# Moving the gate biases into their column block and holding four weight sums behind the low part ahead of them

## The chip, the cores and the metric

The kernel runs on one NeuronCore of a Trainium2 chip. The metric is the device time of one execution in microseconds (us), taken as the median of the runs shown. A profile is one further execution with the hardware profiler on; it lists every instruction of the five engines: TensorE (PE in the rows, with its weight loads as PEld), VectorE (DVE), ScalarE (ACT), GpSimd (POOL) and SyncE (SP, which here only issues transfers).

## The reference, cut to what matters

The program is one layer of an encoder: a half-step feed-forward block, a gated mixer of attention and a Fourier branch, and a second half-step feed-forward block. The change lies in the gated mixer:

```python
u = _rms_norm(h, pre_g)
q, k, v, f, g = jnp.split(u @ w_in, SPLIT_POINTS, axis=-1)
...
y_attn = _blocked_gqa(q, k, v) @ w_attn_o
y_four = _fourier_mix(f) @ w_fourier
gates = jax.nn.sigmoid((g.reshape(b, s, N_BRANCHES, D_MODEL) + b_gate).astype(jnp.float32)).astype(h.dtype)
merged = gates[:, :, 0] * y_attn + gates[:, :, 1] * y_four
return h + _rms_norm(merged @ w_out, post_g)
```

There are 256 tokens, the width is 2048, and all is float32. The gates need `u @ w_in` for 4096 columns and the bias `b_gate`; the Fourier branch ends in a product with `w_fourier`.

## The kernel before, in words

**Products.** Every float32 weight is split into a high part (`whi`, a rounded copy made by ScalarE, line 105) and a low part (`wlo`, the weight minus the high part, made by VectorE, line 106). Each product is then three matmuls: high by high, low by high and high by low (lines 111 to 113). `split` keeps the last low-part instruction that was written down in `latest["V"]`. A weight piece is 128 by 1024 numbers: it is loaded into one of 5 buffers `raw`, and its parts go into rings of 6 buffers `hi` and `lo`.

**Column blocks.** `col_block` multiplies all tokens (two tiles of 128) by 512 columns: 16 steps `kk` of 6 matmuls, into two PSUM tiles `pc`. Other work is hung in between: a list `between`, spread evenly over the 16 steps, and a list `at` of pairs (step, work). `tc.issue_after(ins)` gives an order only: what is traced in the block on the engine of `ins` is queued behind `ins` on that engine, and nothing waits for `ins` to finish. Engines take their instructions strictly in the order in which the program holds them; that order is made beforehand by a scheduler that picks, engine by engine, what it thinks ready, the earlier written first.

**The mixer's middle.** There are eight gate blocks. Blocks 10 to 13 make the gate of the Fourier branch (`mB`), blocks 6 to 9 that of the attention (`zA`). `gate` runs a column block, loads 512 biases into `bg`, and then, for each of the two token tiles, VectorE computes `z` from `pc` and `bg` (line 1110) and ScalarE the sigmoid (line 1111).

A loop over `j` from 0 to 3 then does, in the order written: `gate(6 + j)` with other work hung in between (the Fourier transforms `fourier_parts` for j = 0, the query rotation for j = 1, and in all of them the transposes `turn_q`, whose results are split into `qTh` and `qTl`); `fourier_weights(j)`; `attn_scores` (products `sc`, then the row maximum `mx`, `nmx`, the exponentials `p` on ScalarE, `rinv`); `fourier_out(j)` (products `pf`); and the next query block, or a block of `w_ao` (products `pr`).

`fourier_weights(j)` prepares four weight pieces. For each, VectorE adds the two halves in place (line 1127), makes their difference from it (line 1128), and adds a multiple to `acc` (lines 1135 and 1137); the piece is split, and the ring keeps it until the `pf` matmuls have read it. `fourier_out(j)` needs all four pieces: 6 matmuls of each, then one with `wn` (line 1151) and two with the parts of `acc`.

For j = 0 the Fourier transforms inside the gate block need `zl`, the low part of `zs` (line 988 reads it).

Of the kernel before, what the change touches and what calls it, by code (L numbers as in the profile page):

```python
# [15 lines left out]
ALU = mybir.AluOpType  # L16
AX = mybir.AxisListType

P = 128
# [3 lines left out]
KD = D // P  # L23
F = 5632
NB = 512
# [34 lines left out]
def encoder_layer(  # L60
# [22 lines left out]
    V, A, T = nc.vector, nc.scalar, nc.tensor  # L83

    def load(dst, src):
        nc.sync.dma_start(dst, src)
# [4 lines left out]
    def work(name, shape=None):  # L91
        return wk.tile(shape or [P, NB], F32, tag="wk", name=name)

    def workr(name, shape=None):
        return wk.tile(shape or [P, NB], F32R, tag="wk", name=name)
# [6 lines left out]
    latest = {}  # L102

    def split(hi, lo, src):
        a = A.activation(hi, src, AF.Copy)  # L105
        v = V.tensor_tensor(out=lo, in0=src, in1=hi.bitcast(F32), op=ALU.subtract)  # L106
        latest["A"], latest["V"] = a.ins, v.ins

    def mm3(ps, lh, ll, rh, rl, first, last, onto=False):

        T.matmul(ps, lh, rh, start=first, stop=False, skip_group_check=onto)  # L111
        T.matmul(ps, lh, rl, start=False, stop=False, skip_group_check=onto)  # L112
        return T.matmul(ps, ll, rh, start=False, stop=last, skip_group_check=onto)  # L113
# [34 lines left out]
    def weights(src, spare=None):  # L148

        return [t for load_part in pieces(src, spare) for t in load_part()]  # L150
# [36 lines left out]
    def new_chunk(name):  # L187
        return (chunk.tile([P, 4, S], F32R, tag="ch_hi", name=name + "h"),
                chunk.tile([P, 4, S], F32R, tag="ch_lo", name=name + "l"))

    def new_u(t):
        return tuple(big(f"u{c}{t}", F32R, [P, KD, P]) for c in "hl")

    def col_block(u, w, nb, between=(), at=()):


        at = list(at)
        ps = [pmm.tile([P, NB], F32, tag="mm", name="pc") for _ in range(NT)]
        step = KD / (len(between) + 1)
        done = 0  # L200
        for kg in range(KD // CK):
            wt = weights(w[nb, kg])
            for k in range(CK):
                kk = kg * CK + k
                while at and kk >= at[0][0]:
                    with tc.issue_after(mm.ins):
                        at.pop(0)[1]()
                if done < len(between) and kk >= (done + 1) * step:
                    if between[done]:
                        with tc.issue_after(mm.ins):  # L210
                            between[done]()
                    done += 1
                for t in range(NT):
                    mm = mm3(ps[t][:], u[t][0][:, kk, :], u[t][1][:, kk, :], *wt[k], kk == 0, kk == KD - 1)
        return ps
# [146 lines left out]
    def cbs(a, cb):  # L362
        return a[:, cb * NB:(cb + 1) * NB]
# [413 lines left out]
    u = [new_u(t) for t in range(NT)]  # L777
# [89 lines left out]
    u, rs = nxt.u, nxt.rs  # L867
# [7 lines left out]
    def norm_rope(ps, nm, t):  # L875

        gc, gs = tabs[nm]
        q = work("q")
        ssq = small("ssq4", 4)
        heads = [slice(j * HD, (j + 1) * HD) for j in range(4)]  # L880
        for j, c in enumerate(heads):
            A.activation(q[:, c], ps[t][:, c], AF.Square, scale=rs[t][:, 0:1], accum_out=ssq[:, j:j + 1])
        r = rsqrt(ssq[:], 4, 1.0 / HD, "rh")
        V.tensor_scalar(out=r[:], in0=r[:], scalar1=rs[t][:, 0:1], scalar2=None, op0=ALU.mult)
        for j, c in enumerate(heads):
            A.activation(q[:, c], ps[t][:, c], AF.Copy, scale=r[:, j:j + 1])
        q3 = q[:].rearrange("p (j c) -> p j c", j=4)
        o = work("o")
        V.tensor_tensor(out=o[:].rearrange("p (j c) -> p j c", j=4), in0=q3,
                        in1=gc[:, t, :].unsqueeze(1).to_broadcast([P, 4, HD]), op=ALU.mult)  # L890
        tmp = work("tmp")
        for half in range(2):
            vo = tmp[:].rearrange("p (j a h c) -> p j a h c", j=4, a=2, h=2)[:, :, :, half, :]
            vi = q[:].rearrange("p (j a h c) -> p j a h c", j=4, a=2, h=2)[:, :, :, 1 - half, :]
            vg = gs[:, t, :].rearrange("p (a h c) -> p a h c", a=2, h=2)[:, :, half, :]
            V.tensor_tensor(out=vo, in0=vi, in1=vg.unsqueeze(1).to_broadcast([P, 4, 2, 32]), op=ALU.mult)
        V.tensor_tensor(out=o[:], in0=o[:], in1=tmp[:], op=ALU.add)
        return o
# [203 lines left out]

    def gate(nb, dst, cb, between=(), at=()):

        ps = col_block(u, w_in, nb, between=between, at=at)
        bg = work("bg")
        load(bg[:], b_gate[:, (nb - 6) * NB:(nb - 5) * NB].partition_broadcast(P))
        for t in range(NT):
            z = work("z")
            V.scalar_tensor_tensor(out=z[:], in0=ps[t][:], scalar=rs[t][:, 0:1], in1=bg[:], op0=ALU.mult, op1=ALU.add)  # L1110
            A.activation(cbs(dst[t], cb), z[:], AF.Sigmoid)
# [3 lines left out]
    def fourier_weights(cb):  # L1115


        acc = xpool.tile([P, NB], F32, tag="xt", name="acc")
        nraw, wn = xpool.tile([P, NB], F32, tag="xt", name="nraw"), workr("wn")
        load(nraw[0:NYR, :], w_fn[cb])  # L1120
        A.activation(wn[0:NYR, :], nraw[0:NYR, :], AF.Copy)
        V.tensor_tensor(out=wn[32:40, :], in0=nraw[32:40, :], in1=wn[32:40, :].bitcast(F32), op=ALU.subtract)
        forms = []
        for j in range(4):
            raw = wraw.tile([P, 2, NB], F32, tag="raw", name="raw")
            load(raw[:], w_fo[cb, j].rearrange("p (k c) -> p k c", k=2))
            V.tensor_tensor(out=raw[:, 0, :], in0=raw[:, 0, :], in1=raw[:, 1, :], op=ALU.add)
            V.scalar_tensor_tensor(out=raw[:, 1, :], in0=raw[:, 1, :], scalar=-2.0, in1=raw[:, 0, :],
                                   op0=ALU.mult, op1=ALU.add)
            hi = wring.tile([P, 2, NB], F32R, tag="hi", name="whi")  # L1130
            lo = wring.tile([P, 2, NB], F32R, tag="lo", name="wlo")
            split(hi[:], lo[:], raw[:])
            forms.append((hi, lo))
            if j == 0:
                V.tensor_scalar(out=acc[:], in0=raw[:, 0, :], scalar1=dcol[:, j:j + 1], scalar2=None, op0=ALU.mult)
            else:
                V.scalar_tensor_tensor(out=acc[:], in0=raw[:, 0, :], scalar=dcol[:, j:j + 1], in1=acc[:],
                                       op0=ALU.mult, op1=ALU.add)
        ready[cb] = acc, nraw, wn, forms
# [30 lines left out]
    for k in range(F_AHEAD):  # L1170
        load_f(k)
    kro = []
    gate(10, mB, 0, between=[lambda b=b: fold_tokens(b) for b in range(1, 4)]
         + [lambda t=t: kro.append(norm_rope(pk, "k", t)) for t in range(NT)])
    pq = col_block(u, w_in, 0, at=folds_at(4))
    qs = []
    gate(11, mB, 1, at=folds_at(4), between=[lambda t=t: qs.append(norm_rope(pq, "q", t)) for t in range(NT)])
    gate(12, mB, 2, at=folds_at(4), between=[lambda t=t: turn_k(t) for t in range(NT)])
    gate(13, mB, 3, at=folds_at(4))

# [14 lines left out]
    for j in range(4):  # L1195
        ps, qT = {}, new_chunk("qT")
        turns = [lambda t=t: turn_q(qT, qs, t) for t in range(NT)]
        if j == 0:
            ahead = fourier_parts() + turns
        elif j == 1:  # L1200
            qs = []
            ahead = [lambda t=t: qs.append(norm_rope(pq, "q", t)) for t in range(NT)] + [None] * 2 + turns
        else:
            ahead = turns
        gate(6 + j, zA, j, between=ahead)
        fourier_weights(j)
        for t in range(NT):
            attn_scores(j, qT, t, ps)
        fourier_out(j)
        oT[j] = new_chunk("oT")  # L1210
        parts = attn_parts(j, ps, oT[j])
        if j < 3:
            pq = col_block(u, w_in, j + 1, between=parts)
        if j in (1, 2):
            qs = []
            row_block(oT[j - 1], w_ao, j - 1, yA, j == 1,
                      between=[None] + [lambda t=t: qs.append(norm_rope(pq, "q", t)) for t in range(NT)])
# [175 lines left out]
```

## Time and profile before

| what | value |
|---|---|
| median of 3 runs | 1999.6 us (1998.6 to 2001.35) |
| profiled execution, its own time | 2000.01 us |
| its span in the trace | 1997.9 us |
| what lies around the span | 2.1 us |
| PE busy | 1983.4 us, 99% |
| DVE busy | 1776.0 us, 89% |
| ACT busy | 1301.3 us, 65% |

Busy times are sums over the instructions of an engine. The times at the left of timeline rows are microseconds from the start of the span. "Granted clock" is the TensorE clock as a share of full speed. In a wait row the arrow points from the waiter to what released it. In the loop over `j`, the four stretches in which PE goes from the gate block to the scores begin at about 923, 986, 1062 and 1143 us.

### The profile page before, as it was taken

To read this page: it belongs to the slowest core of one execution; us is meant where nothing else is said; L and a number is where in the kernel's file an instruction comes from. 1 tells how busy PE (TensorE), PEld (TensorE's weight loads), DVE (VectorE), ACT (ScalarE), POOL (GpSimd) and SP (SyncE) were. 2 spreads that over 40 slices of the span, in tenths; PEclk is the share of its full clock that TensorE was granted. 3 is DMA by queue.
4 is the path that set the end of the run, shared out by engine and by line. 5 is a ranking of instruction groups with operands and counts; after the bars stand their busy time and mean duration, and the time that the engine had idled before them with its cause. 6 is when DMAs were issued, how large, how long until landed. Compare 5 with 4: busy or idle time off the path is not lost.

```text
span 1997.9 us, 25756 instructions
## 1 busy us (share of the span) xinstructions
PE 1983.4 (99%) x9146; PEld 1644.7 (82%) x9146; DVE 1776.0 (89%) x2306; ACT 1301.3 (65%) x1860; POOL 84.8 (4%) x94
## 2 busy tenths in 40 slices
PE   9999999999999999999999999999999999999998
PEld 7888888888888888888888888888888888888886
DVE  6999999999999878886877885878999999999996
ACT  7566766767666756556666564656667766677666
POOL 0000000000000010100000000000000000000002
PEclk9999999999999999999999999999999999999999
DMA  9657766677668796854555557565577766677673
GB/s 328 222 177 237 227 221 204 207 242 224 227 203 277 241 302 202 252 181 142 192 193 186 193 166 276 195 216 194 177 230 232 232 209 208 216 232 232 215 259 127
DMA packets 117584, 434.19 MB, mean 217 GB/s; under 512 B 12840, under 2 KB 18992, under 8 KB 106064
## 3 DMA queue, kind: packets, MB, share of 16 engines
q1 hardware_dynamic: 103888, 411.65, 60.4%
q0 software_dynamic: 13568, 20.91, 6.0%
q8 instruction: 71, 1.16, 0.2%
q14 instruction: 57, 0.47, 0.1%
HBM read 409.44 MB, written 6.29 MB: 208 GB/s over the span
## 4 chain that ended last, share of the span: by engine, by line
PE 98%; DVE 1%; DMA 1%; ACT 0%; issue 0%; SPq 0%; DVEq 0%; ACTq 0%
PE pc L112 20%; PE pc L111 20%; PE pc L113 20%; PE pr L113 11%; PE pr L112 11%; PE pr L111 11%; PE pt L184 2%; PE pe L111 0%; PE pe L113 0%; PE pf L112 0%; PE pf L111 0%; PE pf L113 0%; DVE wlo L106 0%; PE pe L112 0%; PE pt L1081 0%; DMA raw<-in_f_gate 0%
## 5 line engine op out<-in xcount | busy, mean ns | idle before, releaser
L106 DVE TENSOR_TENSOR wlo<-raw,whi 128x1024 fp32r<-128x1024 f32 (+1 forms) x567 | 680.7, 1219 | 96.2 <-ACT whi L105 94.1
L105 ACT ACTIVATE whi<-raw 128x1024 fp32r<-128x1024 f32 (+1 forms) x567 | 586.5, 1053 | 252.3 <-PE pc L113 96.1
L112 PE MATMUL pc<-wlo,fh 128*128 128x512 f32 x738 | 287.6, 390 | 0.0
L113 PE MATMUL pc<-whi,fl 128*128 128x512 f32 x738 | 287.6, 390 | 0.0
L111 PE MATMUL pc<-whi,fh 128*128 128x512 f32 x738 | 287.4, 389 | 0.0
L111 PE MATMUL pc<-whi,uh 128*128 128x512 f32 x688 | 271.6, 396 | 1.2 <-ACT uh L838 1.2
L113 PE MATMUL pc<-whi,ul 128*128 128x512 f32 x688 | 269.7, 392 | 0.0
L112 PE MATMUL pc<-wlo,uh 128*128 128x512 f32 x688 | 269.3, 392 | 0.1
L105 ACT ACTIVATE whi<-t 128x1024 fp32r<-128x1024 f32 (+1 forms) x198 | 171.5, 866 | 138.6 <-DVE t L586 133.6
L586 DVE TENSOR_TENSOR t<-raw 128x512 f32<-128x512 f32 (+1 forms) x252 | 208.9, 841 | 14.2 <-DMA raw<-in_f_gu 10.5
L111 PE MATMUL pr<-whi,hTh 128*128 128x512 f32 x544 | 213.6, 393 | 0.0
L113 PE MATMUL pr<-whi,hTl 128*128 128x512 f32 x544 | 212.0, 390 | 0.0
L112 PE MATMUL pr<-wlo,hTh 128*128 128x512 f32 x544 | 211.9, 390 | 0.0
L106 DVE TENSOR_TENSOR wlo<-t,whi 128x1024 fp32r<-128x1024 f32 (+1 forms) x198 | 193.4, 977 | 13.6 <-ACT whi L105 13.3
L105 ACT ACTIVATE w<-raw 128x1024 fp32r<-128x1024 f32 x144 | 151.9, 1055 | 40.4 <-DVE raw L586 35.2
L106 DVE TENSOR_TENSOR w<-raw,w 128x1024 fp32r<-128x1024 f32 x144 | 175.5, 1219 | 0.0
L112 PEld LDWEIGHTS pc<-wlo,fh 128*128 128x128 f32 x738 | 138.6, 188 | 29.1
L111 PEld LDWEIGHTS pc<-whi,fh 128*128 128x128 f32 x738 | 138.6, 188 | 29.0
L113 PEld LDWEIGHTS pc<-whi,fl 128*128 128x128 f32 x738 | 138.6, 188 | 28.8
L111 PEld LDWEIGHTS pc<-whi,uh 128*128 128x128 f32 x688 | 129.7, 188 | 27.9 <-ACT uh L838 2.7
L112 PEld LDWEIGHTS pc<-wlo,uh 128*128 128x128 f32 x688 | 129.6, 189 | 26.8 <-DVE wlo L106 1.7
L113 PEld LDWEIGHTS pc<-whi,ul 128*128 128x128 f32 x688 | 129.4, 188 | 27.0
(350 smaller groups left out, 3183.4 us busy)
## 6 DMA issues: line engine op xcount, KB each, us to landing
raw<-in_f_down SPq DMA_DIRECT2D x176, 512.0 KB, 5.2
raw<-in_f_gu SPq DMA_DIRECT2D x144, 512.0 KB, 4.5
raw<-in_f_gu SPq DMA_DIRECT2D x72, 1024.0 KB, 7.4
raw<-in_w_in SPq DMA_DIRECT2D x112, 512.0 KB, 4.4
raw<-in_f_up SPq DMA_DIRECT2D x32, 512.0 KB, 5.0
raw<-in_w_ao SPq DMA_DIRECT2D x32, 512.0 KB, 3.8
raw<-in_w_out SPq DMA_DIRECT2D x32, 512.0 KB, 4.9
raw<-in_f_gate SPq DMA_DIRECT2D x31, 512.0 KB, 5.8
```

What stands on the lines that cost most here:

```text
L105: a = A.activation(hi, src, AF.Copy)
L106: v = V.tensor_tensor(out=lo, in0=src, in1=hi.bitcast(F32), op=ALU.subtract)
L111: T.matmul(ps, lh, rh, start=first, stop=False, skip_group_check=onto)
L112: T.matmul(ps, lh, rl, start=False, stop=False, skip_group_check=onto)
L113: return T.matmul(ps, ll, rh, start=False, stop=last, skip_group_check=onto)
L184: T.transpose(pt[:, j, :], src[:, j * P:(j + 1) * P], ident[:])
L586: V.tensor_tensor(out=out, in0=a, in1=b, op=ALU.subtract)
```

## The change

Two edits. In `gate`, the load of the biases and the allocation of its buffer are written down inside the column block, at step 8 of 16, and no longer behind it. In `fourier_weights`, the sum of the two halves of each piece is queued on VectorE behind the low-part instruction that was written down last before it (`latest["V"]`). For the first piece of a block that is the last split that was traced inside the gate block; for the other three it is the low part of the piece before. The lines from 1127 on are one line further down in the changed kernel: 1127 becomes 1128, 1128 becomes 1129, 1135 becomes 1136, 1137 becomes 1138, 1150 becomes 1151.

```diff
     def gate(nb, dst, cb, between=(), at=()):
 
-        ps = col_block(u, w_in, nb, between=between, at=at)
         bg = work("bg")
-        load(bg[:], b_gate[:, (nb - 6) * NB:(nb - 5) * NB].partition_broadcast(P))
+        bias = (KD // 2, lambda: load(bg[:], b_gate[:, (nb - 6) * NB:(nb - 5) * NB].partition_broadcast(P)))
+        ps = col_block(u, w_in, nb, between=between, at=sorted([*at, bias], key=lambda a: a[0]))
...
             load(raw[:], w_fo[cb, j].rearrange("p (k c) -> p k c", k=2))
-            V.tensor_tensor(out=raw[:, 0, :], in0=raw[:, 0, :], in1=raw[:, 1, :], op=ALU.add)
+            with tc.issue_after(latest["V"]):
+                V.tensor_tensor(out=raw[:, 0, :], in0=raw[:, 0, :], in1=raw[:, 1, :], op=ALU.add)
             V.scalar_tensor_tensor(out=raw[:, 1, :], in0=raw[:, 1, :], scalar=-2.0, in1=raw[:, 0, :],
                                    op0=ALU.mult, op1=ALU.add)
```

**Place 1: VectorE in the first steps of gate block 6 (j = 0).** The rows run from the two `z` of the block before it to the first low parts of the Fourier transform. Before:

```order
L1110 SCALAR_TENSOR_TENSOR z<-pc,r1r,bg 128x512
L106 TENSOR_TENSOR wlo<-raw,whi 128x1024
L1127 TENSOR_TENSOR raw<-raw 128x512
L106 TENSOR_TENSOR zl<-zs,zh 128x260
L1128 SCALAR_TENSOR_TENSOR raw<-raw 128x512
L106 TENSOR_TENSOR wlo<-raw,whi 128x1024
```

Now:

```order
L1110 SCALAR_TENSOR_TENSOR z<-pc,r1r,bg 128x512
L106 TENSOR_TENSOR wlo<-raw,whi 128x1024
L106 TENSOR_TENSOR zl<-zs,zh 128x260
L106 TENSOR_TENSOR wlo<-raw,whi 128x1024
L106 TENSOR_TENSOR al<-pa,ah 126x260
```

The first sum (line 1127) stood between a low part and `zl`; it and all that follows from it have left this place.

**Place 2: VectorE at the end of gate block 6, from the two `z` on.** Before, the four pieces are done by then, and the rows are scores work and the low parts of the next block's weights:

```order
L106 TENSOR_TENSOR qTl<-pt,qTh 128x4x128
L1110 SCALAR_TENSOR_TENSOR z<-pc,r0r,bg 128x512
L1110 SCALAR_TENSOR_TENSOR z<-pc,r1r,bg 128x512
L1060 TENSOR_REDUCE mx<-sc 128x2
L106 TENSOR_TENSOR wlo<-raw,whi 128x1024
L1122 TENSOR_TENSOR wn<-nraw,wn 8x512
L1061 TENSOR_SCALAR nmx<-mx 128x2
```

Now:

```order
L1110 SCALAR_TENSOR_TENSOR z<-pc,r1r,bg 128x512
L1122 TENSOR_TENSOR wn<-nraw,wn 8x512
L1128 TENSOR_TENSOR raw<-raw 128x512
L1060 TENSOR_REDUCE mx<-sc 128x2
L1129 SCALAR_TENSOR_TENSOR raw<-raw 128x512
L1136 TENSOR_SCALAR acc<-raw,dcol 128x512
L1061 TENSOR_SCALAR nmx<-mx 128x2
L106 TENSOR_TENSOR wlo<-raw,whi 128x1024
L1128 TENSOR_TENSOR raw<-raw 128x512
L1129 SCALAR_TENSOR_TENSOR raw<-raw 128x512
L1138 SCALAR_TENSOR_TENSOR acc<-raw,dcol,acc 128x512
L1068 RECIPROCAL rinv<-rsum 128x2
```

All four pieces, with their sums, differences, `acc` and low parts, now stand behind the two `z`, one piece after the other. For j = 1 it is the same, but that the first sum and difference stand just ahead of the two `z`. On PE the `pf` matmuls keep their place behind three of the four scores products.

**Place 3: VectorE at the end of gate block 9 (j = 3; block 8 is alike).** Before:

```order
L1137 SCALAR_TENSOR_TENSOR acc<-raw,dcol,acc 128x512
L106 TENSOR_TENSOR wlo<-raw,whi 128x1024
L106 TENSOR_TENSOR qTl<-pt,qTh 128x4x128
L1150 SCALAR_TENSOR_TENSOR acc<-nraw,dcol,acc 8x512
L106 TENSOR_TENSOR wlo<-raw,whi 128x1024 x2
L1110 SCALAR_TENSOR_TENSOR z<-pc,r0r,bg 128x512
```

Now:

```order
L1128 TENSOR_TENSOR raw<-raw 128x512
L1129 SCALAR_TENSOR_TENSOR raw<-raw 128x512
L1138 SCALAR_TENSOR_TENSOR acc<-raw,dcol,acc 128x512
L1151 SCALAR_TENSOR_TENSOR acc<-nraw,dcol,acc 8x512
L106 TENSOR_TENSOR wlo<-raw,whi 128x1024
L1110 SCALAR_TENSOR_TENSOR z<-pc,r0r,bg 128x512
```

The four pieces still stand ahead of the two `z`, but now behind the last low part of the gate's own weights; the whole fourth piece, with its sum, now stands between the second `qTl` and the first `z`.

## The prediction

> **What bounds the kernel now.** I read the page first: busy times, then the chain that ended last.
>
> ```profile
> span 1997.9 us, 25756 instructions
> PE 1983.4 (99%) x9146; PEld 1644.7 (82%) x9146; DVE 1776.0 (89%) x2306; ACT 1301.3 (65%) x1860; POOL 84.8 (4%) x94
> PE 98%; DVE 1%; DMA 1%; ACT 0%; issue 0%; SPq 0%; DVEq 0%; ACTq 0%
> ```
>
> TensorE sets the end: 98% of the chain is its own work. Only 1997.9 − 1983.4 = 14.5 us of the span are left to win on it, and every wait given to it lengthens the program one for one. VectorE at 89% has little slack as a mean, so the stretch decides. The table by stages gives, for each window, its length, the busy time of PE, PEld, DVE, ACT and POOL, the granted clock, the DMA share and GB/s; the first row holds gate block 6, the second the scores and `pf` behind it, the third the query block, gate block 7 with its `pf`, and what follows:
>
> ```profile
> 882.00:925.00 43.00, 41.21 (x223) 34.53 (x223) 30.43 (x45) 19.71 (x36) 0.00 (x0) 0.96 0.43 139
> 925.00:960.00 35.00, 35.00 (x179) 29.20 (x178) 26.14 (x38) 26.00 (x56) 0.00 (x0) 1.00 0.55 184
> 960.00:1050.00 90.00, 90.00 (x433) 74.78 (x432) 74.12 (x135) 62.27 (x121) 0.00 (x0) 1.00 0.57 189
> ```
>
> PE loses 1.8 us in the first window and nothing in the others. VectorE has 12.6 us free of 43 inside gate block 6 and 8.9 of 35 behind it. What the waits of PE and of `z` name there (number, us in all, longest):
>
> ```profile
> PE pa L988 <- DVE zl L106: 1.8, 1, 1.8
> DVE z L1110 <- DMA bg<-in_b_gate: 1.4, 2, 1.0
> ```
>
> **Part 1, the biases: 0.** The same number of loads is issued on SP's queue, earlier. It removes at most the 1.4 us that `z` waited for them in all. During both waits PE had other work: its second window shows it full at 35.00 of 35.00 just behind such a `z`. So I take 0; the bounds are −1.4 and +1.0, the latter if a transfer put ahead makes a weight late by one such wait.
>
> **Part 2, place 1: −3.5 us.** VectorE there, then the PE row that waited, then the two windows before and behind it:
>
> ```profile
> 887.23 1.23 DVE L106 TENSOR_TENSOR wlo<-raw,whi 128x1024 fp32r<-128x1024 f32 x1
> 889.94 0.69 DVE L1127 TENSOR_TENSOR raw<-raw 128x512 f32<-128x512 f32 x1 [1.49 <-DMA raw<-in_w_fo]
> 890.55 0.42 DVE L106 TENSOR_TENSOR zl<-zs,zh 128x260 fp32r<-128x260 f32 x1
> 891.49 1.22 DVE L106 TENSOR_TENSOR wlo<-raw,whi 128x1024 fp32r<-128x1024 f32 x1
> 892.62 0.68 DVE L1127 TENSOR_TENSOR raw<-raw 128x512 f32<-128x512 f32 x1
> 893.34 0.69 DVE L1128 SCALAR_TENSOR_TENSOR raw<-raw 128x512 f32<-128x512 f32 x1
> 893.95 0.68 DVE L1127 TENSOR_TENSOR raw<-raw 128x512 f32<-128x512 f32 x1
> 891.02 0.33 PE L988 MATMUL pa<-odd,zl 128*126 128x130 f32 x1 [1.77 <-DVE zl L106]
> 888.38:891.79 3.41, 1.64 (x13) 1.29 (x13) 1.92 (x5) 1.22 (x2) 0.00 (x0) 1.00 0.77 257
> 891.79:895.21 3.42, 3.42 (x16) 3.12 (x16) 3.35 (x5) 1.08 (x3) 0.00 (x0) 0.50 0.41 155
> ```
>
> The first sum waited for its transfer, and `zl` stood behind it. In the changed order `zl` follows the low part of 887.23 at once and is done by about 888.9, ahead of 891.02 − 1.77 = 889.25, where PE began to wait. So 1.77 us go. The window behind the wait ran at half the clock, 3.42 × 0.5 = 1.7 us of work lost; that goes with it. Together −3.5; bounds 0 (something else becomes late there) and −3.5.
>
> **Part 2, place 2, j = 0: +11.1 us.** Before, this preparation lay inside the gate block, under PE's 16 steps. Now all of it is behind the two `z`, and `pf` needs it. Rows of VectorE, of PE and of ScalarE:
>
> ```profile
> 916.45 2.33 DVE L1137 SCALAR_TENSOR_TENSOR acc<-raw,dcol,acc 128x512 f32<-128x512 f32 x3
> 920.56 0.73 DVE L1150 SCALAR_TENSOR_TENSOR acc<-nraw,dcol,acc 8x512 f32<-8x512 f32 x1
> 922.68 0.69 DVE L106 TENSOR_TENSOR qTl<-pt,qTh 128x512 fp32r<-128x512 f32 x1
> 923.29 0.74 DVE L1110 SCALAR_TENSOR_TENSOR z<-pc,r0r,bg 128x512 f32<-128x512 f32 x1
> 923.95 0.74 DVE L1110 SCALAR_TENSOR_TENSOR z<-pc,r1r,bg 128x512 f32<-128x512 f32 x1
> 924.61 0.68 DVE L1060 TENSOR_REDUCE mx<-sc 128x2 f32<-128x512 f32 x1
> 925.21 1.21 DVE L106 TENSOR_TENSOR wlo<-raw,whi 128x1024 fp32r<-128x1024 f32 x1
> 923.24 0.28 PE L111 MATMUL sc<-kT,qTh 128*128 128x256 f32 x1
> 925.39 0.40 PE L111 MATMUL pf<-whi,foTh 128*128 128x512 f32 x1
> 925.62 0.40 PE L112 MATMUL pf<-wlo,foTh 128*128 128x512 f32 x1
> 931.71 0.39 PE L1151 MATMUL pf<-wn,mids 72*128 72x512 f32 x1
> 931.95 0.39 PE L111 MATMUL pc<-whi,uh 128*128 128x512 f32 x1
> 926.98 1.06 ACT L105 ACTIVATE whi<-raw 128x1024 fp32r<-128x1024 f32 x1 [0.87 <-PE pf L113]
> ```
>
> Count from the first `z` (0 = 923.29), with distances from one row to the next where two follow each other: `z` 0.66 each, `mx` 0.6, sum 0.72 to its own difference and difference 0.61 to the next (the three rows around 893), `acc` 2.33 / 3 = 0.78, a low part 1.13 (891.49 to 892.62), a high part 1.06. Two `z` and `wn` (like `mx`) end at 1.9, the first sum at 2.5; `mx` stands next, so the difference ends at 3.9, the high part at 5.0, the first low part at 6.2. From then a piece costs 0.72 + 0.61 + 0.78 + `rinv` or `nmx` 0.1 + `mx` 0.6 + low part 1.14 = 4.0; the high part (1.06) lies under `acc` and `mx` (1.38), so it costs nothing, but if ScalarE is late with it (a table load stands in its queue) each piece grows by up to 1.3. The fourth has `acc` of line 1150 too, 0.73. The fourth low part ends at 6.2 + 4.0 + 4.0 + 4.7 = 18.9, and behind it PE has still some four matmuls of `pf` (0.23 apart) and the one of `wn`: the query block starts at 20.05. Before, PE went from the first score to that block in 931.95 − 923.24 = 8.7 us, 8.9 with one matmul that the changed order pulls ahead. The difference is **11.1**. Below: all of `mx` and `rinv` fall between pieces without delay, −2. Above: 4 × 1.3 = +5.
>
> Queued behind it on VectorE are the low parts of the query block. They need PE's 20.05 at the earliest and are 1.13 each against 2.7 us of PE (12 matmuls) for a weight piece: no term. The four buffers `raw` come free at 6 to 19, so the weights after next land late by as much, but the nearest that depends on the last is wanted some ten microseconds behind the start of the query block: no term either; what a late transfer would cost goes into the upper end.
>
> **Part 2, place 2, j = 1: +8.9 us.** The same, with the first sum and difference ahead of `z`: first low part at 2.5, second 7.9 (its high part waits for the difference, ending at 5.6, and VectorE for both), third 11.9, fourth 16.6, query block 17.8; less 8.9. Bounds −2 and +4 around it.
>
> **Part 2, place 3, j = 2 and j = 3: +2.0 and +2.8.** Here the pieces stay ahead of `z`, but begin behind the last low part of the gate's weights. Rows of VectorE, of PE (the fourth scores product) and of ScalarE:
>
> ```profile
> 1048.11 1.22 DVE L106 TENSOR_TENSOR wlo<-raw,whi 128x1024 fp32r<-128x1024 f32 x1
> 1062.02 0.74 DVE L1110 SCALAR_TENSOR_TENSOR z<-pc,r0r,bg 128x512 f32<-128x512 f32 x1
> 1129.84 1.21 DVE L106 TENSOR_TENSOR wlo<-raw,whi 128x1024 fp32r<-128x1024 f32 x1
> 1142.49 0.74 DVE L1110 SCALAR_TENSOR_TENSOR z<-pc,r0r,bg 128x512 f32<-128x512 f32 x1
> 1068.94 0.39 PE L111 MATMUL sc<-kT,qTh 128*128 128x256 f32 x1
> 1149.40 0.39 PE L111 MATMUL sc<-kT,qTh 128*128 128x256 f32 x1
> 1063.59 1.28 ACT L1111 ACT_TABLE_LOAD   x1
> 1064.88 1.15 ACT L1111 ACTIVATE zA<-z 128x512 f32<-128x512 f32 x2
> 1065.94 0.62 ACT L1121 ACTIVATE wn<-nraw 72x512 fp32r<-72x512 f32 x1
> ```
>
> A piece is sum 0.72, difference 0.69, high part 1.06, low part 1.14, about 3.7 with the gaps; from the end of the gate's last low part, 1049.25, four of them, with `qTl` (0.7) under the last, put the first `z` at 1064.85, against 1062.02. ScalarE has the fourth high part, two of the next block (to 65.6), a table load, the sigmoids 1.15, `wn` 0.6, a second table load 1.3 and the two exponentials (0.9): done at 1070.9. The fourth scores product needs the buffer that they free and stood at 1068.94: **+2.0**. The same for j = 3 from 1131.0: `z` at 1146.1, against 1142.49, exponentials done at 1152.2 against 1149.40: **+2.8**. Bounds 0 (`acc` and the high parts overlap wholly) and 3 or 4.
>
> **The clock: +3.4.** One wait of 1.77 us was followed by one window of 3.42 us at 0.50. The waits at j = 0 and 1 are longer, so at least one such window each: 2 × 1.7. Bounds 0 and +8 (windows within the waits, and behind the 2-us waits at j = 2, 3: five in all).
>
> **Sum.** 11.1 + 8.9 + 2.0 + 2.8 + 3.4 − 3.5 + 0 = +24.7. The profiled execution took 2000.0 us (1997.9 of span and 2.1 around it), 0.4 over the median of the runs; so 1999.6 + 24.7 = 2024.
>
> **Rivals.**
> 1. *The clock stays at half while the waits recur.* Each piece's six matmuls (0.23 apart) are a burst of 1.4 us between waits of 2 to 3 us; if the gate counts the share of busy time, as the window with 1.64 of 3.41 us suggests, it stays at 0.50 from the first wait until a full window: the 8.7 us of PE work at each of j = 0, 1 then take up to twice as long, 17.4 us more, of which I leave a third to two thirds under the next wait: +7 to +12, 2031 to 2036. Against: the burst hides in the wait that follows it.
> 2. *The clock never falls.* Place 2 is no single wait of 11 us but four or five, cut by the bursts of a piece's matmuls; the longest by the steps above is 4.0 − 1.2 = 2.8 us. If such waits are too short for the gate, the clock term goes: −3.4, 2020.6. Against it stands the window at 0.50 behind a wait of 1.77 us. The Trainium skill, "TensorE: Matmul & The Clock Gate", section "Why this matters for your kernels", gives this rule: gaps of an idle PE above some 3 us are to be avoided, since one idle window takes the clock back to half. By it the clock stays full here; the trace disagrees, with 1.77 us before its slow window.
> 3. *Half of it.* VectorE takes ready work between the waits better than I chain it, or one of the two blocks is prepared in time because the engine reaches the held sum before `z` is ready: 2 × 10 goes to 10, 2011 to 2013. For j = 1 the sum's place ahead of `z` speaks for it; against it, that the second `qTl` at 922.7 leaves 0.6 us only.
> 4. *The other side: faster.* If the first sum runs at least 11 us before the first `z` in all four blocks (VectorE's 12.6 us free in the block would then take the four pieces), no `pf` waits and only place 1 counts: 1999.6 − 3.5 = 1996. It decides by where the second `qTl` stands; in the order it is directly ahead of the `z`.
> 5. *No change*: the waits at j = 2, 3 and the gain at place 1 cancel (2.0 + 2.8 − 3.5 = +1.3), with place 2 hidden as in 4.
>
> **How the numbers follow.** Forecast 0.57, rivals 0.15, 0.12, 0.08, 0.05, 0.03. A measurement tells from no change about 0.2%, 4 us: faster 0.05 (rival 4), same 0.03, slower 0.92. The summed bounds of the large terms are −4 and +9, with which the forecast itself reaches from 2016 to 2032; taking in rivals 1 and 2 and cutting rival 3, 2014 to 2034.
>
> **What would show it.** Right: PE's waits list `pf` (lines 111 and 112) behind `whi` and `wlo`, about 10 us at 921 to 942 and as much near 1000; the one of line 988 is gone; the windows behind 925 and near 1000 show PE some 10 us short of full, with a clock under 1.00 in the table of windows there; scores products of blocks 8 and 9 wait 2 to 3 us for `p`. Wrong: first sums that start long before the first `z`, or waits of `pf` under 5 us in a block. The bias rows should no longer release `z`, with no time coming of it.

## The result and the profile after

The changed kernel takes 2020.9 us in the median (2019.8 to 2022.4), against 1999.7 us before; the ratio is 1.0106 (95% interval 1.0091 to 1.0121), so 21.2 us slower, with 18 to 24 us in the interval. The prediction was 2024.

The page of the profiled execution of the changed kernel, in the same rows as before:

```profile
span 2019.8 us, 25750 instructions
PE 1992.9 (99%) x9146; PEld 1647.5 (82%) x9146; DVE 1777.3 (88%) x2306; ACT 1300.4 (64%) x1860; POOL 84.8 (4%) x94
PE 93%; DVE 4%; ACT 1%; DMA 1%; issue 0%; SPq 0%; DVEq 0%; ACTq 0%
```

The instructions that count as busy are the same in number on each engine (the six fewer in the span row are not among them) and VectorE's busy time is nearly the same; the chain that ended last now runs through VectorE for 4% of the span. PE's busy time has grown by 9.5 us though its matmuls are the same: that is mostly the lower clock. The rest of the 21.9 us of span is idle time. The waits of PE (what waited, for what: us in all, times, longest) say where:

```profile
PE pf L111 <- ACT whi L105: 10.3, 5, 3.0
PE pc L111 <- ACT whi L105: 2.0, 2, 1.0
PE pf L112 <- DVE wlo L106: 1.5, 3, 0.5
```

None of these was there before, and the wait of line 988 for `zl` is gone. The list names ScalarE's high parts first, but ScalarE is only the last link; for the first high part of j = 0 it waited itself, for VectorE's difference:

```profile
924.03 1.06 ACT L105 ACTIVATE whi<-raw 128x1024 fp32r<-128x1024 f32 x1 [2.00 <-DVE raw L1129]
```

In the timeline of VectorE behind the two `z` of gate block 6 one piece follows the other almost without a gap (lines as in the changed kernel, one more than before; only the second `qTl`, the first `z`, the four sums and the fourth low part are shown, the rows between them are left out):

```profile
919.35 0.69 DVE L106 TENSOR_TENSOR qTl<-pt,qTh 128x512 fp32r<-128x512 f32 x1 [2.52 <-ACT qTh L105]
919.96 0.74 DVE L1110 SCALAR_TENSOR_TENSOR z<-pc,r0r,bg 128x512 f32<-128x512 f32 x1
922.10 0.69 DVE L1128 TENSOR_TENSOR raw<-raw 128x512 f32<-128x512 f32 x1
926.26 0.69 DVE L1128 TENSOR_TENSOR raw<-raw 128x512 f32<-128x512 f32 x1
930.05 0.69 DVE L1128 TENSOR_TENSOR raw<-raw 128x512 f32<-128x512 f32 x1
934.05 0.68 DVE L1128 TENSOR_TENSOR raw<-raw 128x512 f32<-128x512 f32 x1
937.36 1.21 DVE L106 TENSOR_TENSOR wlo<-raw,whi 128x1024 fp32r<-128x1024 f32 x1
```

The first sum stands 2.1 us behind the first `z`, the sums are 4.2, 3.8 and 4.0 us apart, and the fourth low part ends at about 938.5, 18.5 us behind the first `z`. Ahead of the second `qTl` VectorE stood idle for 2.5 us: it waited for the `qTh` that this `qTl` reads, and the sums stand behind it in its order. PE, meanwhile (the longer waits):

```profile
925.14 1.22 PE L111 MATMUL pf<-whi,foTh 128*128 128x512 f32 x2 [2.92 <-ACT whi L105]
932.93 0.73 PE L111 MATMUL pf<-whi,foTh 128*128 128x512 f32 x2 [1.55 <-ACT whi L105]
936.92 0.73 PE L111 MATMUL pf<-whi,foTh 128*128 128x512 f32 x2 [1.54 <-ACT whi L105]
938.67 0.79 PE L111 MATMUL pc<-whi,uh 128*128 128x512 f32 x1 [1.01 <-ACT whi L105]
```

To see what each block cost, I compare one and the same matmul in both timelines of PE. Before (the first scores product of j = 0; a matmul of the query block behind j = 0; one of the column block behind j = 1; the fourth scores products of j = 2 and 3 stand in the prediction):

```profile
956.53 0.40 PE L112 MATMUL pc<-wlo,uh 128*128 128x512 f32 x1
1039.76 0.39 PE L112 MATMUL pc<-wlo,uh 128*128 128x512 f32 x1
```

and in the changed kernel, with the fourth scores products of j = 2 and 3 too:

```profile
919.91 0.28 PE L111 MATMUL sc<-kT,qTh 128*128 128x256 f32 x1
966.07 0.40 PE L112 MATMUL pc<-wlo,uh 128*128 128x512 f32 x1
1060.81 0.39 PE L112 MATMUL pc<-wlo,uh 128*128 128x512 f32 x1
1090.02 0.39 PE L111 MATMUL sc<-kT,qTh 128*128 128x256 f32 x1
1170.48 0.39 PE L111 MATMUL sc<-kT,qTh 128*128 128x256 f32 x1
```

The shifts are −3.3 at the first scores product (923.24 before), +9.5 behind j = 0, +21.1 behind j = 1, and +21.1 still at j = 2 (1068.94) and j = 3 (1149.40). Ahead of place 1 the changed kernel was already 0.3 us late (the first `z` of the block before gate block 6: 886.13 against 885.87). So place 1 gave 3.6 us, j = 0 took 12.9, j = 1 took 11.5, j = 2 and 3 took nothing. The last 0.8 us of the span's 21.9 came behind the loop over `j`, all of it near 1895 us in the second feed-forward block; single runs of one kernel lie 2 to 3 us apart, and I give it no cause.

The clock, in the table by windows of the changed kernel (length, busy time of PE, PEld, DVE, ACT and POOL, granted clock, DMA share, GB/s):

```profile
919.16:938.71 19.55, 11.48 (x49) 7.66 (x48) 18.49 (x33) 13.72 (x29) 0.00 (x0) 0.91 0.25 80
938.71:942.62 3.91, 3.91 (x10) 3.17 (x11) 3.66 (x5) 3.91 (x9) 0.00 (x0) 0.56 0.71 235
1006.99:1013.82 6.83, 6.22 (x15) 4.86 (x16) 6.40 (x11) 6.83 (x16) 0.00 (x0) 0.50 0.63 208
```

The first row holds all waits of j = 0; VectorE is busy for 18.5 of its 19.6 us. The second and third are the windows behind the last low part of j = 0 and j = 1: full or nearly full of matmuls, at about half the clock. By PE's busy time in them they lose 3.91 × 0.44 = 1.7 and 6.22 × 0.5 = 3.1 us, 4.8 together.

### The profile page after: what moved, and what is told of

Read it like the earlier page. It is cut to its first block, busy times and chain, and to the rows that moved or that the text cites. A ratio compares the mean times of both kernels' runs of the same rounds, so it can differ in the third digit from the quotient of the medians.

```text
span 2019.8 us, 25750 instructions
## 1 busy us (share of the span) xinstructions
PE 1992.9 (99%) x9146; PEld 1647.5 (82%) x9146; DVE 1777.3 (88%) x2306; ACT 1300.4 (64%) x1860; POOL 84.8 (4%) x94
## 4 chain that ended last, share of the span: by engine, by line
PE 93%; DVE 4%; ACT 1%; DMA 1%; issue 0%; SPq 0%; DVEq 0%; ACTq 0%
PE pc L112 19%; PE pc L111 19%; PE pc L113 19%; PE pr L113 10%; PE pr L112 10%; PE pr L111 10%; PE pt L184 2%; DVE wlo L106 1%; ACT whi L105 1%; PE pe L111 0%; PE pe L113 0%; DMA raw<-in_f_gu 0%; PE pe L112 0%; PE pt L1081 0%; DMA raw<-in_w_in 0%
## 5 line engine op out<-in xcount | busy, mean ns | idle before, releaser
L586 DVE TENSOR_TENSOR t<-raw 128x512 f32<-128x512 f32 (+1 forms) x252 | 208.9, 841 | 15.0 <-DMA raw<-in_f_gu 11.2
```

The source lines that it names most:

```text
L586: V.tensor_tensor(out=out, in0=a, in1=b, op=ALU.subtract)
```

## The experiments

**The two edits apart.** First the biases alone: the new `gate`, and `fourier_weights` as before.

```diff
-            with tc.issue_after(latest["V"]):
-                V.tensor_tensor(out=raw[:, 0, :], ...
+            V.tensor_tensor(out=raw[:, 0, :], ...
```

> Only the biases are moved; the first sums are not held. Theory: the biases price nothing, so 1999.7 us, within 2 us of before (the interval holds 1.000); the wait of PE for zl (1.8 us) and its window at half the clock stay, and no z waits for its biases. Rival: the earlier loads shift the weights behind them and carry a part of the loss, then over 2 us slower; or the 1.4 us of waits of z were paid by PE, then 1998.3 us.

Measured: 2000.4 us, ratio 0.9999 (0.9991 to 1.0008). The earlier load costs and brings nothing within 2 us. The wait for `zl` is there (1.4 us). Two details came out otherwise than expected: no window at half the clock follows that wait (the last section returns to this), and one `z` still waited 1.4 us for its biases.

Then the hold alone, with `gate` as before the change.

```diff
-        bg = work("bg")
-        bias = (KD // 2, lambda: load(bg[:], ...))
-        ps = col_block(u, w_in, nb, between=between, at=sorted([*at, bias], key=lambda a: a[0]))
+        ps = col_block(u, w_in, nb, between=between, at=at)
+        bg = work("bg")
+        load(bg[:], ...)
```

> Only the hold; the biases are loaded where they were before. Theory: all of the change's effect is here, 2020 to 2022 us, with the same waits of pf (about 12 us) as in the changed kernel. Rival: the two edits act together (the biases landing while VectorE is on the pieces), then under 2015 us.

Measured: 2020.6 us, ratio 1.0100 (1.0086 to 1.0113), with 9.4 us of waits of `pf` for high parts and 1.7 for low parts (10.3 and 1.5 in the changed kernel). The hold carries the whole effect.

**Block by block.** The sums are held in some blocks only; the biases stay moved. In the code of `fourier_weights`, `cb` is what the text calls j, the gate block from 0 to 3, and `j` is the piece.

```diff
-            with tc.issue_after(latest["V"]):
+            with tc.issue_after(latest["V"]) if cb >= 2 else contextlib.nullcontext():
```

> Biases moved, and the sums held in the last two gate blocks only (j = 2, 3). Theory after the trace of the changed kernel: the hold costs nothing there, 1999.7 us within 2 us, with the zl wait still there. Rival, the prediction's own terms: +2.0 and +2.8, 2004.5 us, with waits of the fourth scores product for the exponentials.

Measured: 2000.4 us, ratio 0.9999 (0.9990 to 1.0008), with no wait of the scores products. The prediction's terms for j = 2 and 3, 4.8 us together, lie outside this interval.

With `cb == 0` in place of `cb >= 2`:

> Biases moved, sums held in the first gate block alone (j = 0). Theory: that block's share as the trace of the changed kernel gives it, 12.9 us lost at the scores and pf less 3.6 us gained at zl, +9.3: 2009.7 us, with about 8 us of waits of pf. Rival: the waits of the second block are partly a consequence of the first (weights that land late), then this kernel carries more than 13 us; or the gain at zl is not real, then +12.9, 2013 us.

Measured: 2011.0 us, ratio 1.0051 (1.0038 to 1.0065), +10.3 us. The waits of `pf` are those of the first block alone:

```profile
PE pf L111 <- ACT whi L105: 6.0, 3, 2.9
PE pf L112 <- DVE wlo L106: 1.1, 2, 0.5
```

With `cb == 1`:

> Biases moved, sums held in the second gate block alone (j = 1). Theory: the two blocks add up, so this is the change (+21.2) less the run held at j = 0 alone (+11.6 by medians, +10.3 by the ratio): +9.6 to +11.5, 2009 to 2011 us, with about 6 us of waits of pf, and the zl wait there. Rival (the second block is worse because the first ran late): under 2007 us.

Measured: 2009.9 us, ratio 1.0044 (1.0030 to 1.0059), +8.8 us, a little under what was expected but with an interval (+6.0 to +11.8) that holds it. `pf` waited 3.8 us for high parts, not some 6; the wait for `zl` is there (1.1 us). The two blocks together make 19.1 us against 21.2 of the change, which the intervals allow. So the second block is not slow because the first is.

**The chain of four, or one late piece?** Only the first piece of j = 0 and j = 1 is held.

```diff
-            with tc.issue_after(latest["V"]):
+            with tc.issue_after(latest["V"]) if cb < 2 and j == 0 else contextlib.nullcontext():
```

> Biases moved, and only the first piece of j = 0 and j = 1 held; pieces 2 to 4 may go ahead of it. Theory (the serial chain of four pieces behind z costs, not the place of the first): sums and differences of the other three leave the chain, three times 0.72 + 0.61 less, so some 4 to 5 us less per block: 2009 to 2012 us. Rival (one piece late is enough, pf waits for it all the same): 2019 to 2021 us.

Measured: 2008.8 us, ratio 1.0040 (1.0026 to 1.0054), +8.0 us. The waits of `pf` for high parts fall from 10.3 to 4.3 us. VectorE now makes three low parts in one go, since the other pieces' sums and differences were done inside the gate block:

```profile
PE pf L111 <- ACT whi L105: 4.3, 2, 2.9
927.04 3.50 DVE L106 TENSOR_TENSOR wlo<-raw,whi 128x1024 fp32r<-128x1024 f32 x3
```

More than half of the loss hangs on `latest["V"]` being the piece before for pieces 2 to 4: each waits for the whole of its predecessor. The saving at place 2 is rather larger than these times say, since in this kernel the free pieces stand in the chain of the Fourier transform again, where PE waits 1.2 and 0.2 us for `oh` and `ol`, as in the next run.

**The gain at `zl` by itself.** One sum is held, the first of j = 0, and only behind the low part `zl` for which PE waited.

```diff
         split(zh[:], zl[:], zs[b])
+        latest.setdefault("zl", latest["V"])
...
-            with tc.issue_after(latest["V"]):
+            with tc.issue_after(latest["zl"]) if (cb, j) == (0, 0) else contextlib.nullcontext():
```

> Biases moved; of all sums only the very first (first piece, j = 0) is held, and behind the low part zl of the first Fourier transform, not behind the second qTl. Theory: place 1 keeps its gain and place 2 loses nothing, -3.5 us: 1996.2 us, with no wait of PE over 0.5 us in the loop over j and the clock full behind 889. Rival: zl is not what PE waits for last, another low part or the first sum's transfer turns up late in its place, then 1998 to 2000 us.

Measured: 2000.8 us, ratio 1.0001 (0.9992 to 1.0009): nothing. The wait for `zl` is gone, and another stands 6 us further on. Rows of PE and of VectorE in this kernel:

```profile
897.37 0.33 PE L111 MATMUL pb<-oh,dcs 126*128 126x128 f32 x1 [0.98 <-ACT oh L105]
897.93 0.33 PE L112 MATMUL pb<-ol,dcs 126*128 126x128 f32 x1 [0.23 <-DVE ol L106]
892.05 0.69 DVE L1129 TENSOR_TENSOR raw<-raw 128x512 f32<-128x512 f32 x1 [0.71 <-DMA raw<-in_w_fo]
...
896.33 0.42 DVE L106 TENSOR_TENSOR al<-pa,ah 126x260 fp32r<-126x260 f32 x1
896.78 0.27 ACT L105 ACTIVATE ah<-pa 8x130 fp32r<-8x130 f32 x1 [3.45 <-DVE al L106]
```

The sums and differences now stand between `zl` and `al`; ScalarE's next step of the transform waited 3.45 us for `al`, its `oh` came late, and PE waited 1.2 us in all, with a window at half the clock behind it (899.05 to 902.46). The rival was right, though 2000.8 lies a little above its range: it is not the sum ahead of `zl` alone that costs; the batch of sums and differences one step further on in this chain of small steps costs as much.

**A version for this place.** All four sums of j = 0 are held, each behind one early mark and not behind one another: the low part `foTl` of the first Fourier channels. No other block is held.

```diff
         split(foT[0][0][:, j, :], foT[0][1][:, j, :], pb[:, 0:2 * P])
+        latest.setdefault("mark", latest["V"])
...
-            with tc.issue_after(latest["V"]):
+            with tc.issue_after(latest["mark"]) if cb == 0 else contextlib.nullcontext():
```

> Biases moved; in the first gate block all four sums are held, not one behind the other, but each behind the low part of the first Fourier channels (foTl), early in the block; the other blocks as before the change. Theory: nothing that PE waits for early in the block stands behind a sum, and VectorE still has some 25 us for the four pieces ahead of z: no wait of PE over 0.5 us in the loop over j and -3.5 us, 1996.9 us. Rival: the pieces end too late and pf waits, or another part of the transform turns late in zl's place as in the run held behind zl: 1999 to 2003 us.

Measured: 1997.1 us, ratio 0.9987 (0.9978 to 0.9996), 2.6 us faster than before (0.8 to 4.4), where −3.5 was expected. It beats both kernels. Its window over gate block 6, and the first sums and the first `z` in it:

```profile
886.00:921.00 35.00, 34.84 (x199) 29.03 (x197) 25.89 (x41) 16.01 (x31) 0.00 (x0) 1.00 0.46 148
896.58 0.42 DVE L106 TENSOR_TENSOR foTl<-pb,foTh 128x256 fp32r<-128x256 f32 x1
896.91 1.28 DVE L1129 TENSOR_TENSOR raw<-raw 128x512 f32<-128x512 f32 x2
...
920.34 0.74 DVE L1111 SCALAR_TENSOR_TENSOR z<-pc,r0r,bg 128x512 f32<-128x512 f32 x1
```

The sums start 23 us ahead of the first `z`, and PE is all but full at a clock of 1.00.

**The clock by itself.** Matmuls that nobody reads are put on PE in the changed kernel, so that it is busy while `pf` waits. First 40 of them, with no order given:

```diff
+            for _ in range(FILL[cb][j]):
+                T.matmul(fill[:], foT[0][0][:, j, P:2 * P], u[0][0][:, 0:4, :], start=True, stop=True)
             mm3(pe[:], ...
```

> The changed kernel with 40 further matmuls on PE that nobody reads (0.23 us each), put ahead of the pf matmuls that wait in j = 0 and j = 1, in about the length of those waits; VectorE and ScalarE keep their order. Theory (the windows at half the clock behind the waits cost time of their own): with PE kept busy the clock stays at 1.00 there, and the windows behind the last wait of each block (about 1.2 and 2.9 us) come back, 2016 to 2018 us. Rival (the slow windows lie under the waits, or the matmuls only add their time): 2021 us or more.

Measured: 2021.8 us, ratio 1.0105 (1.0092 to 1.0119): a miss. Two of the waits that stayed show why:

```profile
932.90 0.73 PE L111 MATMUL pf<-whi,foTh 128*128 128x512 f32 x2 [1.54 <-ACT whi L105]
1006.83 0.73 PE L111 MATMUL pf<-whi,foTh 128*128 128x512 f32 x2 [1.54 <-ACT whi L105]
```

The scheduler had put all 40 ahead of the third pieces, so these waits were no shorter than in the changed kernel, and the clock fell behind them (934.1 to 944.4 and 1009.2 to 1012.6 us). This run does not tell the theories apart. So once more, with each batch kept behind the `pf` of the piece before and ahead of its own:

```diff
+                with tc.issue_after(mm.ins) if mm else contextlib.nullcontext():
+                    mm = T.matmul(fill[:], ...)
+            with tc.issue_after(mm.ins) if mm else contextlib.nullcontext():
+                mm3(pe[:], ...)
+                mm = mm3(po[:], ...)
```

> The changed kernel again with matmuls that nobody reads (67 of them), but now each batch is kept ahead of the pf matmuls of its piece, so that every wait of pf for a high part in j = 0 and j = 1 is filled. Theory (only the slow windows behind the last wait of a block cost time: 938.7 to 942.6 us and 1007.0 to 1013.8 us of the changed kernel's profile, half of each, 2.0 and 3.1 us): no window below 1.00 behind the last pf, 2016 us (2015 to 2018), the pf themselves as late as before. Rival (the waits alone cost, the clock is nothing): 2020.5 to 2022 us.

(There are 68.) Measured: 2017.9 us, ratio 1.0085 (1.0070 to 1.0100), so +17.0 us where the change has +21.2. The same stretches as above, in this kernel:

```profile
919.16:938.71 19.55, 18.59 (x91) 14.47 (x89) 17.77 (x31) 13.44 (x28) 0.00 (x0) 1.00 0.24 81
1006.99:1013.82 6.83, 6.83 (x33) 5.61 (x33) 5.95 (x9) 6.83 (x17) 0.00 (x0) 1.00 0.77 248
```

The clock is at 1.00 throughout, and the kernel got faster by having more to do. VectorE was no earlier: the fourth low part of j = 0 still ends about 18.5 us behind the first `z`. The first `z` of j = 1 comes 69.8 us behind that of j = 0 instead of 71.4, and the one of j = 2 comes 89.4 us behind that of j = 1 instead of 92.3: 1.6 and 2.9 us back, against 1.7 and 3.1 read from the windows. The intervals of the two ratios overlap, so the size by times alone is weak; windows and distances agree with it.

## Why the prediction was right, step by step

- **The biases, 0.** Right; in the changed kernel no `z` waited for its biases.
- **Place 1, −3.5.** Right in size: −3.6 in the changed kernel. The reason was too narrow. I named one late step, `zl`; the changed kernel gains there because all work on the four pieces has left the stretch. Moving only the sum off `zl` gave nothing.
- **Place 2, j = 0, +11.1.** Measured 12.9, of which 1.7 is the clock behind the last low part: 11.2. The steps were right too: the fourth low part was forecast to end 18.9 us behind the first `z` and ended at 18.5, a piece was forecast at 4.0 and took 3.8 to 4.2. That PE would have to wait through all of it holds as forecast, and so does the one matmul of the query block that goes ahead of the last `pf`.
- **Place 2, j = 1, +8.9.** Measured 11.5, less 3.1 of clock: 8.4.
- **Place 3, +2.0 and +2.8.** Wrong, both are 0. The failed step is "from the end of the gate's last low part, 1049.25": I took the time of that low part from the trace of before, where a sum, a difference and an `acc` stood directly ahead of it on VectorE. The change moves these behind it, so it comes earlier. The three rows ahead of it before, then its row and that of the first `z` in the changed kernel:

```profile
1046.12 0.68 DVE L1127 TENSOR_TENSOR raw<-raw 128x512 f32<-128x512 f32 x1
1046.84 0.69 DVE L1128 SCALAR_TENSOR_TENSOR raw<-raw 128x512 f32<-128x512 f32 x1
1047.45 0.75 DVE L1137 SCALAR_TENSOR_TENSOR acc<-raw,dcol,acc 128x512 f32<-128x512 f32 x1
1067.32 1.23 DVE L106 TENSOR_TENSOR wlo<-raw,whi 128x1024 fp32r<-128x1024 f32 x1 [1.49 <-ACT whi L105]
1083.66 0.73 DVE L1110 SCALAR_TENSOR_TENSOR z<-pc,r0r,bg 128x512 f32<-128x512 f32 x1
```

  Less the shift of 21.1 this is 1046.2 instead of 1048.11; with it the first `z` is only 1083.66 − 21.1 − 1062.02 = 0.5 us late, not 2.8, and the exponentials are done before the fourth scores product needs their buffer.
- **The clock, +3.4.** The mechanism was right, the size too small: 4.8 by the windows, 4.2 by the difference of the two ratios. I counted one slow window per block; there was one behind j = 0 and two behind j = 1. Slow windows that lie under the waits cost nothing that shows, since PE would have waited anyway. They also hide waits: I named about 10 us of waits in each block, and PE stood idle for 8.1 us at j = 0 (19.55 − 11.48) and 6.0 at j = 1 (28.98 busy of the 35 us from 985 to 1020); matmuls at half the clock fill the rest.
- **The sum.** 0.3 − 3.6 + 11.2 + 8.4 + 0 + 0 + 4.8 = 21.1, with the 0.3 from ahead of place 1. The prediction's 24.7 was too high by the 4.8 of place 3; the clock's 1.4 went the other way, and that the two offset each other in part was luck. The range has a slip in its working: bounds of −4 and +9 around 2024 give 2020 to 2033, not 2016 to 2032. The measured 2020.9 lies in either.
- **The rivals.** The clock did not stay at half, though the share of busy time does count (see the last section): in the middle of the waits of j = 0 a window with little more than half of PE's time busy ran at 1.00, and so did the one behind it:

```profile
931.88:935.29 3.41, 1.84 (x6) 0.97 (x6) 3.29 (x7) 2.17 (x6) 0.00 (x0) 1.00 0.38 115
935.30:938.71 3.41, 0.86 (x4) 0.34 (x3) 3.41 (x8) 3.41 (x9) 0.00 (x0) 1.00 0.41 144
```

  It did not stay full either, though no single wait is longer than 3.0 us: the window behind these two ran at half, with no single wait over 1.55 us in them. The rule of the Trainium skill ("TensorE: Matmul & The Clock Gate", section "Why this matters for your kernels"), to avoid idle gaps of PE above some 3 us because one idle window takes the clock back to half, is not enough here: much shorter gaps did the same. Half of the loss is what came with the chain taken apart, which the change does not do. The other side, the sums early enough ahead of `z`, is what the version held behind `foTl` does, and there the forecast of that rival (1996) is 1.1 us from the measured 1997.1; in the change itself the sums stand behind the `z`, and that rival did not come about.

## What to carry to other kernels

A hold behind "the last one written" takes its meaning from what was written last: in gate blocks 8 and 9 that was the last low part of the gate's own weights, and it cost nothing; in blocks 6 and 7 it was the last of the interleaved work, at the end of the block; and in a loop it makes the pieces a chain. Name the instruction to hold behind, early enough that the work still lies under PE. And when an edit moves work behind a reference point, take the time of that point again: it may be the moved work that had made it late.

## What the runs showed of the hardware

The clock falls for about 3.4 us behind waits of PE that are far shorter than that, and not behind all of them. In the run held at j = 2 and 3 alone, one wait of 1.33 us stands in the first of these two windows, and the second runs at half:

```profile
888.72:892.14 3.42, 2.09 (x21) 1.88 (x19) 2.45 (x4) 1.08 (x2) 0.00 (x0) 1.00 0.75 258
892.14:895.55 3.41, 3.41 (x13) 2.83 (x11) 3.34 (x7) 1.14 (x4) 0.00 (x0) 0.50 0.62 209
```

In the run with the biases alone a wait of 1.41 us at the same place was followed by none:

```profile
891.10 0.33 PE L988 MATMUL pa<-odd,zl 128*126 128x130 f32 x1 [1.41 <-DVE zl L106]
887.36:890.77 3.41, 2.33 (x13) 1.75 (x11) 2.28 (x4) 2.67 (x5) 0.00 (x0) 1.00 0.76 235
890.77:894.18 3.41, 3.08 (x23) 2.86 (x24) 3.38 (x6) 1.08 (x3) 0.00 (x0) 1.00 0.52 155
```

So neither the length of a wait alone nor its place in the program decides. The traces show what does, at least in part. The moments at which the granted clock changes lie a whole number of 3.413 us apart in each of the twelve traces; in the changed kernel the slow stretches begin at 925.05, 938.71, 1000.15 and 1006.97 us, which is 4, 18 and 2 such windows from one to the next. The windows are fixed, then, and do not begin with a wait. The wait of 1.33 us lies wholly inside one window; that of 1.41 us begins at 889.7 and ends at 891.1, across the border at 890.77, and leaves both windows fuller.

I counted all windows of this grid that ran at full clock in the twelve traces. Each one in which PE was busy for 1.55 us or less was followed by one at half, and none with 2.33 us or more. Between the two both occur (the 1.84 us at 931.88 in the changed kernel were followed by a full one, the 2.09 us at 888.72 above by one at half), so busy time as the profile gives it is not the whole rule. A window at half was followed by another where PE was busy for 2.98 us of it or less, and by a full one from 3.26 us on.

For a forecast it means that a wait of 1 to 2 us costs either itself or itself and 1.7 us more.
